# Scores of a half's last key tile from whole F32 operands in layer A's attention

## The chip, the core and the metric

The kernel runs on one core of one Trainium2 chip. The metric is the device time of one execution in microseconds (us); lower is better. Engines are named as the profile names them: PE (TensorE matmuls), PEld (TensorE weight loads), DVE (VectorE), ACT (ScalarE), POOL (GpSimd) and SP (SyncE, which here only issues DMAs).

## The reference

The program is a two-layer decoder trunk on one sequence of 1024 tokens, width 1024, in F32. Layer A is an mLSTM mixer, layer B a dilated sliding-window attention; the change lies in layer A. Cut to what is computed there (4 heads of width 512; b is the running sum of the log forget gates):

```
xc = silu(causal_dwconv(xm, conv_w, conv_b))
q = headwise(xc, wq); k = headwise(xc, wk); v = headwise(xm, wv)
sc  = einsum('bhld,bhsd->bhls', qc, kc) * w_intra      # causal, decayed by the gates
num = ... + einsum('bhls,bhsv->bhlv', sc, vc)
den = ... + sc.sum(-1)
h   = num / max(|den|, exp(-m))
y   = (group_norm(sigmoid(o) * h) * gn_g + skip * xc) * silu(z)
x   = layer_norm(ALPHA * x + y @ w_out)
```

The reference walks over the sequence in chunks with a carried state; the kernel computes the same as one causal attention over the 1024 tokens.

## The kernel before, in words

Almost every product of the kernel is made by `mm3` (lines 95 to 99): both operands have been split by `split` (lines 91 to 93) into a part h in the type fp32r (an ACT cast, line 92) and a rest l (a subtraction on DVE, line 93), and three matmuls h*h, h*l and l*h are added up in PSUM (lines 97, 98, 99). At some places of layer B the kernel instead gives TensorE whole F32 operands in one matmul instruction (lines 1240, 1242, 1290, 1321).

`layer_a_attend` is layer A's attention. It goes through 8 steps, (head, half) with 4 heads and 2 halves of 512 queries. A step has nj = 4 (first half) or 8 (second half) key tiles of 128 tokens. For each key tile j

- `scores` (line 787) multiplies, over the head's 4 channel tiles cc, the 128 keys (the conv output xc, split) with the queries (split; the weights of q and k are folded into the query side by `prep_q`). Because of causality only query columns from `lo * 128` on are needed, with lo = max(0, j - 4 * half): tiles of 512 columns, and at the end of each half one each of 384, 256 and 128 columns. Then ACT makes the exponentials (line 801), DVE multiplies (803), the result is split (805), and a running sum is kept (807, 809).
- `values` (line 812) multiplies the score tile with the values, 3 matmuls of 512 columns for each query block.

Scores run two key tiles ahead of values. At the end of a step `prep_q` (line 763) makes the next step's queries: for each of 4 channel tiles, three matmuls into PSUM bank 6 or 7, then the split from PSUM. `gather` and `norm` (lines 819, 830) finish the step's numerator, with 4 activations of ACT at line 854. `finish` (line 856) is called in the following step: it transposes h (line 867), scales the conv output in place by skip (ACT, line 869), adds the transposed h (DVE, line 870) and multiplies with the gate (POOL, line 871). The conv output that `finish` works on is a whole F32 copy, `self.xc`, one tile of 128 x 1024 for each of the 16 channel tiles; four of them are loaded at line 892, in each first half's iteration j == 1.

Tiles of SBUF are numbered slots; a slot's next user waits until the last reader of the one before has ended. Slots 50 and 51 are used before the attention (weights of the output gate) and after it (`w_raw` of `layer_a_out`, line 959: the raw tiles of w_out, loaded at line 964, turn about in 50 and 51). The attention itself does not use them.

The order of instructions on each engine, DMA issues on SP included, is fixed when the program is built: the tile framework's planner (line 1667, `schedule_with_timeline_sim=True`) takes the program order as priority, plays the program through with durations of its own, and lets an engine that would be idle go ahead with work that is later in the program. On the chip each engine follows the order so found and waits by semaphores.

Of the kernel before, what the change touches and what calls it, by code (L numbers as in the profile page):

```python
# [18 lines left out]
P = 128  # L19
# [6 lines left out]
HC = NC_A // HA  # L26
# [10 lines left out]
def f(ap):  # L37
    return ap.bitcast(F32)
# [22 lines left out]
class Kernel:  # L61
# [674 lines left out]
    def layer_a_attend(self):  # L736
        nc, cp = self.nc, self.cp
        V, A, G, T = nc.vector, nc.scalar, nc.gpsimd, nc.tensor
        xc_slots = ((40, 41, 42, 43), (8, 9, 10, 11))
        v_slots = (0, 1, 2, 3, 12, 13, 14, 15)  # L740
        q_slots = (44, 45, 46, 52)
        tos = Ring(7, 49)
        es, shl, hsl, pbs = Ring(5, 6), Ring(33, 34, 35), Ring(36, 37), Ring(4, 39)
        pS, pT = Ring(4, 5), Ring(6, 7)
# [1 line left out]
        xcs, vts, qs = {}, {}, {}  # L746

        def prep_x(hd, half, ccs=range(HC)):
            for cc in ccs:
                hl = self.slot(xc_slots[half][cc], (P, 2, 512), F32R)  # L750
                nc.sync.dma_start(f(hl), self.dram["xp", hd * HC + cc, half])
                xcs[hd, cc, half] = hl[:, 0], hl[:, 1]

        def prep_v(hd, half, js=range(4)):
            for j in js:
                j += 4 * half
                h, l = self.pair(v_slots[j])
                nc.sync.dma_start(f(l), self.dram["v", hd][j * P:j * P + P, :])
                self.nc.scalar.copy(h, f(l))
                G.tensor_tensor(l, f(l), f(h), op=ALU.subtract)  # L760
                vts[hd, j] = h, l

        def prep_q(hd, half):
            At = self.slot(48, (P, 2, 512), F32R)
            nc.sync.dma_start(f(At), self.dram["A", hd // 2][:, :, (hd % 2) * 512:(hd % 2) * 512 + 512])
            for cc in range(HC):
                ps = self.bank(pT)
                cs = slice(cc * P, cc * P + P)
                h, l = xcs[hd, cc, half]
                self.mm3(ps, At[:, 0, cs], At[:, 1, cs], h, l, True, True)  # L770
                qh, ql = self.pair(q_slots[cc])
                self.split(qh, ql, ps)
                qs[hd, cc, half] = qh, ql

        accs = {}
# [11 lines left out]
        def scores(hd, half, j, st):  # L787
            lo = max(0, j - 4 * half)
            ps = self.bank(pS)
            for cc in range(HC):  # L790
                kh, kl = xcs[hd, cc, j // 4]
                ks = slice((j % 4) * P, (j % 4) * P + P)
                qh, ql = qs[hd, cc, half]
                self.mm3(ps[:, lo * P:], kh[:, ks], kl[:, ks], qh[:, lo * P:], ql[:, lo * P:],
                         cc == 0, cc == HC - 1)
            e = self.slot(es, (P, 2, 512))
            E, sc = e[:, 0], e[:, 1]
            for i in range(lo, 4):
                ig = 4 * half + i
                src = st["pbm"] if ig == j else st["pb"]  # L800
                A.activation(E[:, i * P:i * P + P], src[:, i * P:i * P + P], AF.Exp, bias=self.bias[:, hd, ig, j:j + 1])  # L801
            cs = slice(lo * P, 512)
            V.scalar_tensor_tensor(sc[:, cs], ps[:, cs], SCALE_A, E[:, cs], op0=ALU.mult, op1=ALU.mult)
            sh, sl = self.pair(shl)
            self.split(sh[:, cs], sl[:, cs], sc[:, cs])
            if j == 0:
                V.tensor_copy(st["acc"], sc)
            else:
                (G if half else V).tensor_tensor(st["acc"][:, cs], st["acc"][:, cs], sc[:, cs], op=ALU.add)
            return lo, sh, sl  # L810

        def values(hd, half, j, st, sc):
            lo, sh, sl = sc
            vh, vl = vts[hd, j]
            for i in range(lo, 4):
                ts = slice(i * P, i * P + P)
                self.mm3(st["num"][i], sh[:, ts], sl[:, ts], vh, vl, j == 0, j == 4 * half + i)
# [38 lines left out]
        def finish(hd, half, st, c2):  # L856

            sz = self.slot(38, (P, 2, 512))
            for ii in range(2):
                c = hd * HC + 2 * c2 + ii  # L860
                self.last_load = nc.sync.dma_start(sz[:, ii], self.dram["z", c][:, 512 * half:512 * half + 512])
            for ii in range(2):
                cc = 2 * c2 + ii
                c = hd * HC + cc
                pt = self.bank(pT)
                for i in range(4):
                    T.transpose(pt[:, i * P:i * P + P], st["h"][i][:, cc * P:cc * P + P], self.ident)  # L867
                xcv = self.xc[c][:, 512 * half:512 * half + 512]
                A.activation(xcv, xcv, AF.Copy, scale=self.skip[:, c:c + 1])
                V.scalar_tensor_tensor(xcv, pt, self.gng[:, c:c + 1], xcv, op0=ALU.mult, op1=ALU.add)  # L870
                G.tensor_tensor(xcv, xcv, sz[:, ii], op=ALU.mult)  # L871
# [11 lines left out]
        for n, (hd, half) in enumerate(steps):  # L883
            st["num"] = [self.bank(i) for i in range(4)]
            nj = 4 * half + 4
            last = n + 1 == len(steps)
            nxt = None
            for j in range(nj):
                if j == 1 and half == 0:
                    for c in range(HC * hd, HC * hd + HC):  # L890
                        t = self.slot((20, 21, 22, 23, 24, 25, 26, 27, 16, 17, 18, 19, 28, 29, 30, 31)[c])
                        nc.sync.dma_start(t, self.dram["xc", c])
                        self.xc.append(t)
                if j + 2 < nj:
                    ahead.append(scores(hd, half, j + 2, st))
                if not last:
                    if half == 0 and j < 2:
                        prep_x(*steps[n + 1], (2 * j, 2 * j + 1))
                        prep_v(*steps[n + 1], (2 * j, 2 * j + 1))
                    if half and j in (2, 3):  # L900
                        prep_x(*steps[n + 1], (2 * j - 4, 2 * j - 3))
                    if half and j in (4, 5):
                        prep_v(*steps[n + 1], (2 * j - 8, 2 * j - 7))
                    if j + 2 == nj:
                        prep_q(*steps[n + 1])
                values(hd, half, j, st, ahead.pop(0))
                if prev and j in (2, 3):
                    finish(*prev, j - 2)
            gather(hd, half, st)
            if not last:  # L910
                nst = begin(*steps[n + 1])
                ahead.append(scores(*steps[n + 1], 0, nst))
            norm(hd, half, st)
            prev = hd, half, st
            if not last:
                ahead.append(scores(*steps[n + 1], 1, nst))
                st = nst
# [753 lines left out]
```

## Time and profile before

| | us |
|---|---|
| three timed runs | 2014.91, 2022.83, 2025.81 |
| their median | 2022.83 |
| the profiled execution, its own time | 2016.23 |
| its span, first to last instruction | 2014.5 |
| PE busy in the span | 1963.6 (97%) |
| DVE busy | 1444.0 (72%) |
| ACT busy | 993.1 (49%) |
| POOL busy | 154.0 (8%) |

How to read it: the span is cut into instructions with a start, a duration and, where an engine stood idle before one, what released it. [...] The profile names tiles without numbers: `s` is any slot, `b` any PSUM bank, `dc` the scratch copy of the conv output. A helper's line stands for all its callers; so most matmuls are on lines 97 to 99, casts on 92 and subtractions on 93. The attention's steps lie between about 500 and 790 us, and the projection with w_out follows.

### The profile page before, as it was taken

To read this page: it belongs to the slowest core of one execution; us is meant where nothing else is said; L and a number is where in the kernel's file an instruction comes from. 1 tells how busy PE (TensorE), PEld (TensorE's weight loads), DVE (VectorE), ACT (ScalarE), POOL (GpSimd) and SP (SyncE) were. 2 spreads that over 40 slices of the span, in tenths; PEclk is the share of its full clock that TensorE was granted. 3 is DMA by queue.
4 is the path that set the end of the run, shared out by engine and by line. 5 is a ranking of instruction groups with operands and counts; after the bars stand their busy time and mean duration, and the time that the engine had idled before them with its cause. 6 is when DMAs were issued, how large, how long until landed. Compare 5 with 4: busy or idle time off the path is not lost.

```text
span 2014.5 us, 26553 instructions
## 1 busy us (share of the span) xinstructions
PE 1963.6 (97%) x9512; PEld 1627.5 (81%) x9512; DVE 1444.0 (72%) x2851; ACT 993.1 (49%) x1988; POOL 154.0 (8%) x127
## 2 busy tenths in 40 slices
PE   8999999999999999999999999999999999999997
PEld 6788888788888888878788888877887788888776
DVE  8778787675467776457867765776568987776888
ACT  5455555535645543343524542565255456675621
POOL 0110000012145343000000000000000000000000
PEclk9999999999999999999999999999999999999999
DMA  4345465456754543516121143125335632224753
GB/s 170 133 168 199 160 219 183 151 164 237 269 204 158 198 157 113 185 63 241 53 74 52 54 149 112 66 102 178 109 104 196 235 105 84 85 95 149 274 199 126
DMA packets 116477, 300.65 MB, mean 149 GB/s; under 512 B 13493, under 2 KB 31349, under 8 KB 116345
## 3 DMA queue, kind: packets, MB, share of 16 engines
q1 hardware_dynamic: 116344, 298.95, 42.5%
q8 instruction: 75, 1.23, 0.2%
q14 instruction: 58, 0.47, 0.1%
HBM read 206.32 MB, written 92.59 MB: 148 GB/s over the span
## 4 chain that ended last, share of the span: by engine, by line
PE 76%; DVE 12%; DMA 6%; ACT 3%; issue 2%; SPq 0%; POOL 0%; DVEq 0%; ACTq 0%
PE b L97 23%; PE b L99 23%; PE b L98 23%; DVE s L93 3%; PE b L592 1%; ACT s L92 1%; DMA s<-df 1%; PE b L1267 1%; DMA s<-in_w_qk 1%; DVE s L230 1%; DVE s L141 1%; PE b L598 1%; PE b L867 1%; DVE s L1406 1%; PE b L1290 1%
## 5 line engine op out<-in xcount | busy, mean ns | idle before, releaser
L98 PE MATMUL b<-s,s 128*128 128x512 f32 (+3 forms) x2720 | 1036.8, 383 | 2.1 <-DVE s L93 2.1
L99 PE MATMUL b<-s,s 128*128 128x512 f32 (+3 forms) x2720 | 1023.5, 383 | 6.0 <-DVE s L93 6.0
L97 PE MATMUL b<-s,s 128*128 128x512 f32 (+2 forms) x2720 | 1003.6, 387 | 25.7 <-ACT s L92 21.9
L93 DVE TENSOR_TENSOR s<-s,s 128x512 fp32r<-128x512 f32 (+2 forms) x702 | 508.2, 739 | 285.9 <-ACT s L92 280.3
L92 ACT CAST s<-s 128x512 fp32r<-128x512 f32 (+3 forms) x706 | 436.0, 638 | 544.2 <-PE b L99 316.5
L97 PEld LDWEIGHTS b<-s,s 128*128 128x128 f32 x2720 | 512.8, 189 | 130.5 <-ACT s L92 30.0
L99 PEld LDWEIGHTS b<-s,s 128*128 128x128 f32 x2720 | 511.7, 189 | 108.1 <-DVE s L93 11.5
L98 PEld LDWEIGHTS b<-s,s 128*128 128x128 f32 x2720 | 513.7, 189 | 99.4 <-DVE s L93 4.4
L230 DVE TENSOR_TENSOR s<-s,b 128x512 f32<-128x512 f32 x132 | 89.9, 682 | 31.9 <-PE b L99 30.5
L1253 ACT ACTIVATE s<-s,nmax 128x128 f32<-128x128 f32 (+1 forms) x192 | 84.4, 441 | 44.0 <-DVE nmax L1251 43.6
L93 DVE TENSOR_TENSOR s<-b,s 128x512 fp32r<-128x512 f32 (+1 forms) x96 | 51.6, 553 | 34.9 <-ACT s L92 31.2
L557 DVE SCALAR_TENSOR_TENSOR s<-s,c_convw,s 128x512 f32<-128x512 f32 (+3 forms) x96 | 71.2, 753 | 3.5 <-ACT s L554 3.2
L224 DVE TENSOR_TENSOR s<-s,b 128x512 f32<-128x512 f32 x88 | 59.6, 680 | 17.3 <-PE b L99 12.6
L314 DVE TENSOR_TENSOR s<-s,b 128x512 f32<-128x512 f32 x100 | 63.2, 680 | 8.0 <-PE b L99 6.2
L801 ACT ACTIVATE s<-s,k 128x128 f32<-128x128 f32 x144 | 47.2, 392 | 42.3 <-DVE s L93 19.3
L310 DVE TENSOR_TENSOR s<-s,s 128x1024 f32<-128x1024 f32 x40 | 49.7, 1246 | 19.9 <-DMA s<-in_w_o 9.9
L1249 DVE CUSTOM_DVE_ANT_0 s<-b,k 128x128 f32<-128x128 f32 (+1 forms) x192 | 57.2, 344 | 7.5 <-PE b L99 5.5
L243 DVE TENSOR_TENSOR s<-s,s 128x512 f32<-128x512 f32 x44 | 30.3, 689 | 42.9 <-DMA s<-in_w_qk 20.5
L92 ACT CAST s<-b 128x512 fp32r<-128x512 f32 (+1 forms) x96 | 43.9, 480 | 24.1 <-PE b L99 13.7
L760 POOL TENSOR_TENSOR s<-s 128x512 fp32r<-128x512 f32 x32 | 43.7, 1381 | 76.7 <-DMA s<-dv 45.5
L1200 DVE SCALAR_TENSOR_TENSOR s<-s,s 128x512 fp32r<-128x512 f32 x48 | 42.4, 884 | 9.9 <-ACT s L1199 9.5
L871 POOL TENSOR_TENSOR s<-s,s 128x512 f32<-128x512 f32 x32 | 42.7, 1351 | 64.5 <-DVE s L870 48.8
(179 smaller groups left out, 1476.6 us busy)
## 6 DMA issues: line engine op xcount, KB each, us to landing
s<-in_w_qk SPq DMA_DIRECT2D x48, 512.0 KB
s<-in_w_out SPq DMA_DIRECT2D x40, 512.0 KB
dp<-s SPq DMA_DIRECT2D x32, 512.0 KB
s<-dp SPq DMA_DIRECT2D x32, 512.0 KB
s<-in_w_z SPq DMA_DIRECT2D x24, 512.0 KB
s<-in_w_v SPq DMA_DIRECT2D x24, 512.0 KB
dg<-s SPq DMA_DIRECT2D x24, 512.0 KB
s<-dg SPq DMA_DIRECT2D x24, 512.0 KB
```

The source lines that it names most:

```text
L92: self.nc.scalar.copy(h, src)
L93: self.last_split = (l_eng or self.nc.vector).tensor_tensor(l, src, f(h), op=ALU.subtract)
L97: mm(ps, lh, rh, start=start, stop=False, skip_group_check=skip)
L98: mm(ps, lh, rl, start=False, stop=False, skip_group_check=skip)
L99: mm(ps, ll, rh, start=False, stop=stop, skip_group_check=skip)
L224: V.tensor_tensor(o, p, q, op=add)
L230: V.tensor_tensor(o, p[lane][rows], q[lane][rows], op=add)
L310: eng.tensor_tensor(o[j], p[j], q[j], op=op)
L314: V.tensor_tensor(o, p, q, op=add)
L557: V.scalar_tensor_tensor(u[i][:, lo:o + 512], xm[i][:, lo - s:o + 512 - s], convw[:, c, 3 - s:4 - s], u[i][:, lo:o + 512], op0=ALU.mult, o ...
L1249: V.tensor_tensor_reduce(out=dst, in0=sc, in1=bias, op0=ALU.add, op1=ALU.max, scale=1.0, scalar=-3e38, accum_out=mx[:, b:b + 1])
L1253: self.last_exp = A.activation(res[b][0], res[b][0], AF.Exp, bias=nm[:, b:b + 1], accum_out=stat[:, 1, g, b:b + 1])
```

## The change

The last key tile of each half, the one with 128 query columns (lo == 3), is no longer computed by `mm3` from split operands. For each of the 4 channel tiles one matmul multiplies the whole F32 keys, read from `self.xc`, with a whole F32 copy of the last 128 query columns. That copy is new: `prep_q` writes it from PSUM by one ACT copy of 128 x 128 after each channel tile's split, into a tile in slots 50 and 51, turn about by step. Because the whole keys must be there earlier, the four loads of line 892 are put into iteration j == 0. All other score tiles stay as they were.

```diff
-        q_slots = (44, 45, 46, 52)
+        q_slots, q_whole = (44, 45, 46, 52), Ring(50, 51)
...
             nc.sync.dma_start(f(At), self.dram["A", hd // 2][:, :, (hd % 2) * 512:(hd % 2) * 512 + 512])
+
+            qs[hd, half] = self.slot(q_whole, (P, HC, P))
             for cc in range(HC):
...
                 self.split(qh, ql, ps)
+                nc.scalar.copy(qs[hd, half][:, cc], ps[:, 384:512])
                 qs[hd, cc, half] = qh, ql
...
                 qh, ql = qs[hd, cc, half]
+                if lo == 3:
+                    T.matmul(ps[:, 384:512], self.xc[hd * HC + cc][:, j * P:j * P + P], qs[hd, half][:, cc],
+                             start=(cc == 0), stop=(cc == HC - 1))
+                    continue
                 self.mm3(ps[:, lo * P:], kh[:, ks], kl[:, ks], qh[:, lo * P:], ql[:, lo * P:],
                          cc == 0, cc == HC - 1)
...
-                if j == 1 and half == 0:
+                if j == 0 and half == 0:
                     for c in range(HC * hd, HC * hd + HC):
```

## The prediction

> **What bounds the kernel now.** I read the page's busy table first, then the stretches around the attention, then who waited for whom on PE there, and last the timelines at the places that those name. From the page, the waits between 470 and 830 us, and two stretches (a first-half step and what follows the last score tile; columns: length, then busy us and count of PE, PEld, DVE, ACT, POOL, the granted clock, the DMA share and GB/s):
>
> ```profile
> PE 1963.6 (97%) x9512; PEld 1627.5 (81%) x9512; DVE 1444.0 (72%) x2851; ACT 993.1 (49%) x1988; POOL 154.0 (8%) x127
> ```
> ```profile
> PE b L97 <- ACT s L92: 3.9, 5, 0.9
> ```
> ```profile
> 665.10:712.90 47.80, 46.97 (x241) 39.13 (x240) 35.15 (x77) 25.75 (x59) 23.61 (x19) 1.00 0.40 138
> 775.20:800.00 24.80, 23.88 (x127) 19.83 (x126) 14.73 (x41) 4.91 (x7) 7.96 (x7) 1.00 0.28 94
> ```
>
> PE is the bound, in the attention too: it is busy for 46.97 of 47.80 us at full clock, while ACT has half its time free. What PE loses there is a handful of waits, 3.9 us in five, all for an ACT cast. So the change must be judged by two things: how much PE time a score tile costs, and what happens to those few waits.
>
> **The tile's price.** The first row of the old tile and the two rows behind its last, and the nearest relative of the new one, a group of whole F32 matmuls in layer B (start, duration):
>
> ```profile
> 541.65 0.23 PE L97 MATMUL b<-s,s 128*128 128x128 f32 x1
> ...
> 542.94 0.45 PE L97 MATMUL b<-s,s 128*128 128x512 f32 x1
> 543.23 0.39 PE L98 MATMUL b<-s,s 128*128 128x512 f32 x1
> ```
> ```profile
> 1497.18 0.39 PE L99 MATMUL b<-s,s 128*128 128x512 f32 x1
> 1497.41 1.05 PE L1321 MATMUL b<-s,s 128*128 128x128 f32 x8
> 1498.21 0.48 PE L97 MATMUL b<-s,s 128*128 128x512 f32 x1
> 1498.53 0.40 PE L98 MATMUL b<-s,s 128*128 128x512 f32 x1
> ```
> ```profile
> L1321 PE MATMUL b<-s,s 128*128 128x128 f32 x128 | 16.8, 274 | 0.0
> ```
>
> A 512-column matmul in a stream takes 0.23 us (1497.18 to 1497.41). The old tile's 12 matmuls run from 541.65 to 542.94; the 512-column matmul behind them takes 0.29 instead of 0.23, so they cost 1.29 + 0.06 = 1.35 us. Line 1321 is executed 64 times (8 heads, 2 banks, 4 products), and the profile counts 128: a whole F32 matmul leaves two records. The x8 is thus one bank's four products, as many as the new tile has: 1497.41 to 1498.21, and the matmul behind takes 0.32, so 0.80 + 0.09 = 0.89 us. Both come to 0.11 us for each record. The saving is 1.35 - 0.89 = 0.46 us a tile; there is one such tile in each of 8 steps, so 3.7 us of PE time, which is 0.18%.
>
> [...]
>
> **What of it stays.** PE's waits of the first-half steps, one of them with its chain (the chain of waits, in order of time; the x1 of line 97 is the score tile in question):
>
> ```profile
> 553.49 0.97 PE L97 MATMUL b<-s,s 128*128 128x512 f32 x3 [0.81 <-ACT s L92]
> 604.28 0.50 PE L97 MATMUL b<-s,s 128*128 128x512 f32 x1 [0.92 <-ACT s L92]
> 675.22 0.50 PE L97 MATMUL b<-s,s 128*128 128x512 f32 x1 [0.83 <-ACT s L92]
> 738.50 0.50 PE L97 MATMUL b<-s,s 128*128 128x512 f32 x1 [0.83 <-ACT s L92]
> ```
> ```profile
> 665.11 0.22 PE L97 MATMUL b<-s,s 128*128 128x128 f32 x1
> ```
> ```profile
> 661.37 0.80 PE b L834 x8
> ...
> 670.15 0.28 DVE s L803
> ...
> 670.88 1.28 ACT s L801 x4
> 672.15 2.83 ACT s L854 x4
> 674.98 0.20 ACT s L92
> 675.18 0.04 issue
> 675.22 0.50 PE b L97
> ```
>
> Step (2, 0)'s last tile is on PE from 665.11, over by about 666.5, and waits in its bank until DVE comes to it at 670.15: DVE works off the norm that PE released at 661.37, ACT then does four exponentials and the four activations of line 854, and only then the cast on which PE waits. A tile that ends 0.46 us earlier moves none of this; PE merely waits 0.46 us longer. So steps (1, 0), (2, 0) and (3, 0), where the chain starts at the norm each time, keep nothing. The four second-half tiles are different: behind each of them PE runs without a wait to the next norm, and the next chain starts at that norm. They keep 4 x 0.46 = 1.84 us.
>
> Step (0, 0) has another chain:
>
> ```profile
> 533.42 1.32 ACT s L869 x2
> 534.74 1.04 ACT s L652 x2
> ...
> 539.46 7.60 DMA do<-s
> ...
> 550.52 2.45 ACT s L801 x8
> ```
> ```profile
> L869 ACT ACTIVATE s<-s,c_skip x32: 706/712/727, 486.8 to 546.1; 128x512 f32<-128x512 f32 x32
> L892 SPq DMA_DIRECT2D s<-dc x16: 320/380/1122, 482.9 to 536.8; - x16
> ```
>
> All 32 in-place scalings of line 869 are done before 546.8, far ahead of their program order, as soon as the copies of line 892 have landed. With the change a scaling may not run before the score tile that reads the unscaled keys, so all 32 move behind their tiles. The chain of step (0, 0) then loses the pieces of line 869 ahead of line 652: 1.3 us in this chain, out of which come at most two of the new copies. I count the wait of 0.81 and the tile's 0.46 as saved here, 1.27 us; the bounds are 0 and 1.27.
>
> **What it adds.** Copies: 4 a step, 32 in all. The nearest row is a copy of the same size from PSUM:
>
> ```profile
> L1278 ACT COPY pw<-b x48: 258/267/376, 1094.6 to 1816.7; 128x128 f32<-128x128 f32 x40, 128x256 f32<-128x256 f32 x8
> ```
>
> So 4 x 0.267 = 1.07 us of ACT a step. The bank is not held longer: the subtraction from PSUM begins when the cast ends and is the longer of the two. The moved scalings bring 4 x 0.71 = 2.85 us a step. In the stretch from 665.10 ACT is busy for 25.75 of 47.80 us, so the 7.8 us of two steps fit in; but ACT works in its fixed order, and before the casts of steps (1, 0) to (3, 0) it has PE waiting. Bounds for each of these three: nothing, if the new work stands in ACT's gaps, and 1.07 + 2.85 = 3.9 us, if all of it stands ahead of the cast and no gap takes any. I take one copy, 0.27, near the lower end, since the scalings are the lowest in priority there and the gaps in that stretch are
>
> ```profile
> 668.39 0.69 ACT L801 ACTIVATE s<-s,k 128x128 f32<-128x128 f32 x2 [1.84 <-DVE s L93]
> 669.40 0.40 ACT L801 ACTIVATE s<-s,k 128x128 f32<-128x128 f32 x1 [0.31 <-DVE s L93]
> 670.88 1.28 ACT L801 ACTIVATE s<-s,k 128x128 f32<-128x128 f32 x4 [0.66 <-DVE s L93]
> ```
>
> 2.81 us together, about four scalings. That is +0.8 us.
>
> The loads of line 892 cost nothing where they go: SP issues them by 536.8, the first reader is the tile at 541.65, the others come later. Their move past a step's loads of keys and values is one in the program only, as SP has them ahead of these already. The second-half tile reads columns 896 to 1023, `finish` of the first half writes 0 to 511: no wait.
>
> Slots 50 and 51 cost something of another kind. Now the first two w_out tiles are loaded into them ahead of the attention; with the change the first must wait for step (3, 0)'s last tile, ahead of the wait at 738.50, and the second for step (3, 1)'s:
>
> ```profile
> 497.20 0.33 SPq L964 DMA_DIRECT2D s<-in_w_out  x1
> 501.59 0.33 SPq L964 DMA_DIRECT2D s<-in_w_out  x1
> ```
> ```profile
> 776.47 0.27 PE L99 MATMUL b<-s,s 128*128 128x128 f32 x1
> 796.22 1.03 PE L867 MATMUL b<-c_ident,s 128*128 128x128 f32 x8
> ```
> ```profile
> L92 ACT CAST s<-s 128x1024 fp32r<-128x1024 f32 x4 | 4.2, 1052 | 1.8 <-PE b L99 1.8
> ```
>
> PE goes through the first three w_out tiles, 18 matmuls each, right before the transposes at 796.22, so it needs the second at 796.22 - 36 x 0.23 = 787.9, or 2 us earlier by the savings. A 512 KB transfer took 7.60 us in the chain above, the cast 1.05: 776.7 + 7.6 + 1.05 = 785.4. It just fits; I take 0, with 0 to 2 us as bounds. What is queued behind that load on SP are later w_out tiles, whose parts go into slots that the attention holds to its end.
>
> **The sum.** -1.84 - 1.27 + 0.8 = -2.3 us: 2016.23 - 2.3 = 2013.9 for an execution like the profiled one. That one lies 6.6 us below the median; on the median it is 2022.83 - 2.3 = 2020.5, 0.11% down. About 0.5%, 10 us, is what a measurement of this kernel can tell from no change.
>
> **The rivals.**
> *ACT's order (slower).* The copies and scalings of a step stand ahead of the cast for which PE waits, in all four first-half steps: 4 x 3.9 = 15.7 us, less the 1.84 kept: +13.8, 2036.7. It decides once more than the 2.81 us of gaps is put in front of the cast. For it speaks that ACT is in these chains already, against it the low priority. 0.08.
>
> [...]
>
> *All waits gone (faster).* With ACT free of the scalings until 542 and PE ahead, the planner finds an order without the four waits: -3.7 - 3.4 = -7.1, 2015.7. 0.14.
>
> [...] 0.03.
>
> *Another order elsewhere.* The planner sees other durations and may reorder later stages, or the second w_out tile comes late: a few us either way, seldom 10. 0.15.
>
> The forecast has 0.60. The runs before spread over 10.9 us, so even there a median may stray past 10 us: 0.04 of the 0.60 and 0.04 of the 0.14 I count as faster, with 0.02 of the other orders: faster 0.10. Slower: 0.07 of the first rival and 0.03 of the other orders, 0.10. The rest, 0.80, is within 0.5%. The range: the lowest run less 2.3 is 2012.6, less 7.1 is 2007.8; the highest less 2.3 is 2023.5, with four passes 2029.8. I take 2009 to 2030; most of the first rival is left out.
>
> **What would show it.** Right: 64 records of whole matmuls in the attention with about 0.11 us each, 8 groups of 0.8 us from first start to the next; line 869 spread over the steps up to 790; PE's wait at 553 gone, those near 604, 675 and 738 between 0.9 and 1.6; the second w_out load right after the last tile, and no PE wait before the first transposes of the tail. Wrong: a tile over 1.3 us; a PE wait of several us behind a cast in first-half steps; PE waiting for w_out near 785; or a difference that lies after 830, where nothing was changed but the order.

## The result, and the profile after

The changed kernel takes 2025.96 us (median of 22 runs, 2022.05 to 2032.75), the kernel before 2021.74 beside it (22 runs, 2014.91 to 2027.49). The ratio is 1.0024, with a 95% interval of 1.0015 to 1.0034: slower by about 4.9 us, where 2.3 us less were forecast.

The tile became what was forecast. From the timeline of PE in the kernel after (start, duration), and its group (count, busy us, mean ns):

```profile
544.59 1.06 PE L798 MATMUL b<-s,s 128*128 128x128 f32 x8
545.40 0.47 PE L97 MATMUL b<-s,s 128*128 128x512 f32 x1
545.72 0.39 PE L98 MATMUL b<-s,s 128*128 128x512 f32 x1
```
```profile
L798 PE MATMUL b<-s,s 128*128 128x128 f32 x64 | 9.1, 274 | 0.0
```

Four products leave 8 records and take 0.81 us from first start to the next; the matmul behind takes 0.32 instead of 0.23. (The prices are distances of starts, because the records of neighbours overlap: the one at 545.72 is 0.39 us long, and the next starts at 545.95.) That is 0.90 us for a tile, against the 0.89 forecast, and 64 records in all.

So the time must be lost elsewhere, and it is lost in the attention. The norm of the last step starts at 791.53 us, before it was 785.74 (in a second trace of the kernel before 788.99). The stretch from 480 to 880 us holds the attention and what follows at once. Its row for the kernel before, for the second trace of that, and for the kernel after (length, busy us and count of PE, PEld, DVE, ACT, POOL, granted clock, DMA share, GB/s):

```profile
480.00:880.00 400.00, 395.15 (x1937) 331.48 (x1936) 259.31 (x516) 191.10 (x381) 119.92 (x95) 1.00 0.53 184
```
```profile
480.00:880.00 400.00, 394.70 (x1932) 330.62 (x1931) 259.50 (x513) 192.35 (x386) 122.73 (x97) 1.00 0.52 182
```
```profile
480.00:880.00 400.00, 390.68 (x1883) 324.67 (x1882) 242.99 (x508) 195.12 (x413) 120.10 (x95) 1.00 0.53 182
```

PE stands idle for 9.3 us of these 400, where it stood for 4.9 and 5.3. The waits that the prediction named (553, 604, 675, 738) are gone. In their place, from PE's timeline after, each with what ended the idle time:

```profile
542.39 0.48 PE L97 MATMUL b<-s,s 128*128 128x512 f32 x1 [2.15 <-ACT s L92]
...
600.62 0.67 PE L97 MATMUL b<-s,s 128*128 128x512 f32 x2 [0.73 <-ACT s L92]
...
659.34 0.91 PE L97 MATMUL b<-s,s 128*128 128x512 f32 x3 [0.70 <-ACT s L92]
...
666.94 0.50 PE L97 MATMUL b<-s,s 128*128 128x512 f32 x1 [1.07 <-DMA s<-dA]
...
725.89 0.92 PE L97 MATMUL b<-s,s 128*128 128x512 f32 x3 [0.69 <-ACT s L92]
...
729.77 0.68 PE L97 MATMUL b<-s,s 128*128 128x512 f32 x2 [0.99 <-ACT s L92]
```

From 600 us on these are no longer the waits for the split of a score tile after the norm. They stand in the making of the next step's queries, and in four of these five PE goes on when ACT has cast a query: at 659.34, 0.05 us after the end of the cast that starts at 658.71. (The one at 666.94 is for the load of the query weights.) What ACT does around 659, first before, then after:

```profile
654.76 0.62 ACT L759 CAST s<-s 128x512 fp32r<-128x512 f32 x1 [2.72 <-DMA s<-dv]
655.29 0.58 ACT L92 CAST s<-b 128x512 fp32r<-128x512 f32 x1
...
656.65 0.57 ACT L92 CAST s<-b 128x512 fp32r<-128x512 f32 x1
657.78 0.59 ACT L92 CAST s<-b 128x512 fp32r<-128x512 f32 x1 [0.56 <-PE b L99]
659.70 0.59 ACT L92 CAST s<-b 128x512 fp32r<-128x512 f32 x1 [1.33 <-PE b L99]
661.90 0.62 ACT L759 CAST s<-s 128x512 fp32r<-128x512 f32 x1 [1.61 <-DMA s<-dv]
```
```profile
656.22 0.56 ACT L92 CAST s<-b 128x512 fp32r<-128x512 f32 x1
658.18 0.62 ACT L759 CAST s<-s 128x512 fp32r<-128x512 f32 x1 [1.40 <-DMA s<-dv]
658.71 0.58 ACT L92 CAST s<-b 128x512 fp32r<-128x512 f32 x1
659.19 0.27 ACT L775 COPY s<-b 128x128 f32<-128x128 f32 x1
660.09 0.62 ACT L759 CAST s<-s 128x512 fp32r<-128x512 f32 x1 [0.63 <-DMA s<-dv]
...
663.60 0.27 ACT L775 COPY s<-b 128x128 f32<-128x128 f32 x1 [0.59 <-DVE s L93]
```

Before, the four query casts (`s<-b`) stand together, and ACT waits for PE. After, casts of the values (line 759), which wait for their loads, and the new copies stand between them, and PE waits for ACT. The copies wait too. The group over the attention (us in total, times, longest):

```profile
ACT s L775 <- DVE s L93: 5.5, 13, 0.9
```

In this trace none of the 32 copies begins before DVE's subtraction from the same bank has ended, and ACT's queue stands with it: 16 of them begin 0.03 us after that end, the others later. The one at 663.60, for instance, follows a subtraction that runs from 662.88 for 0.69 us. What keeps the two from running side by side was not shown.

The last piece is the clock. The stretch after those waits, and matmuls in it:

```profile
660.00:670.00 10.00, 8.90 (x41) 7.03 (x40) 5.95 (x18) 3.86 (x9) 3.06 (x3) 0.87 0.44 155
670.00:680.00 10.00, 10.00 (x52) 8.62 (x52) 5.38 (x19) 9.27 (x24) 1.40 (x1) 0.96 0.07 26
```
```profile
668.03 0.63 PE L97 MATMUL b<-s,s 128*128 128x512 f32 x1
668.45 0.63 PE L98 MATMUL b<-s,s 128*128 128x512 f32 x1
668.88 0.63 PE L99 MATMUL b<-s,s 128*128 128x512 f32 x1
```

At a granted clock of 0.87 and 0.96 these 20 us lose 10 x 0.13 + 10 x 0.04 = 1.3 + 0.4 = 1.7 us by estimate; the matmuls stand 0.43 us apart instead of 0.23. In the trace of before no stretch between 480 and 880 had less than 1.00.

To add this up, a stretch of equal work is needed: from the start of ACT's first split of a query (526.84 and 529.23 us before, 527.46 after) to the start of DVE's first row of the product with w_out (861.21 and 864.81, 866.92). Its rows for the kernel before, the second trace of that, and the kernel after:

```profile
526.84:861.21 334.37, 329.52 (x1647) 277.11 (x1646) 219.71 (x451) 154.81 (x319) 115.70 (x92) 1.00 0.50 175
529.23:864.81 335.58, 330.28 (x1647) 277.27 (x1646) 220.31 (x452) 154.73 (x319) 116.67 (x92) 1.00 0.50 175
527.46:866.92 339.46, 330.14 (x1615) 274.54 (x1614) 209.49 (x451) 173.71 (x375) 116.17 (x93) 0.99 0.51 175
```

After, it is 3.9 to 5.1 us longer, which is about the whole loss; what follows it takes 1153.3 and 1156.0 us before and 1155.0 after. PE's idle time in it rises by 4.2 us (9.3 against the mean of 4.9 and 5.3), and the clock takes 1.7. PE's busy time without the clock's 1.7 us falls only by 1.1 to 1.8 us (to 328.4), where eight tiles should spare 8 x 0.45 = 3.6 us. What took the other 2 us or so of busy time was not found.

### The profile page after: what moved, and what is told of

Same layout as the page of the kernel before. It is cut to its first block, busy times and chain, and to the rows that moved or that the text cites. A ratio compares the mean times of both kernels' runs of the same rounds, so it can differ in the third digit from the quotient of the medians.

```text
span 2021.9 us, 26520 instructions
## 1 busy us (share of the span) xinstructions
PE 1966.1 (97%) x9480; PEld 1626.3 (80%) x9480; DVE 1433.3 (71%) x2851; ACT 996.8 (49%) x2020; POOL 154.0 (8%) x127
## 4 chain that ended last, share of the span: by engine, by line
PE 74%; DVE 12%; DMA 9%; ACT 2%; issue 2%; SPq 0%; POOL 0%; DVEq 0%; ACTq 0%
PE b L97 23%; PE b L99 23%; PE b L98 23%; DVE s L93 3%; DMA s<-in_w_out 1%; PE b L592 1%; DMA s<-df 1%; ACT s L92 1%; DMA s<-in_w_qk 1%; PE b L1274 1%; DMA ds<-s 1%; DMA s<-dv 1%; PE b L598 1%; DVE s L1256 1%; PE b L874 1%
## 5 line engine op out<-in xcount | busy, mean ns | idle before, releaser
L98 PE MATMUL b<-s,s 128*128 128x512 f32 (+3 forms) x2688 | 1029.1, 385 | 5.0 <-DVE s L93 4.7
L97 PE MATMUL b<-s,s 128*128 128x512 f32 (+3 forms) x2688 | 999.9, 389 | 29.2 <-ACT s L92 25.0
L99 PE MATMUL b<-s,s 128*128 128x512 f32 (+3 forms) x2688 | 1014.7, 384 | 4.9 <-DVE s L93 4.8
L92 ACT CAST s<-s 128x512 fp32r<-128x512 f32 (+2 forms) x706 | 435.9, 638 | 568.2 <-PE b L99 343.4
L97 PEld LDWEIGHTS b<-s,s 128*128 128x128 f32 x2688 | 507.0, 189 | 135.8 <-ACT s L92 34.8
L98 PEld LDWEIGHTS b<-s,s 128*128 128x128 f32 x2688 | 508.3, 189 | 104.7 <-DVE s L93 10.0
L99 PEld LDWEIGHTS b<-s,s 128*128 128x128 f32 x2688 | 505.7, 189 | 106.8 <-DVE s L93 9.6
L314 DVE TENSOR_TENSOR s<-s,b 128x512 f32<-128x512 f32 x100 | 63.0, 680 | 12.2 <-PE b L99 10.7
```

The costliest lines, as they stand in the source:

```text
L92: self.nc.scalar.copy(h, src)
L97: mm(ps, lh, rh, start=start, stop=False, skip_group_check=skip)
L98: mm(ps, lh, rl, start=False, stop=False, skip_group_check=skip)
L99: mm(ps, ll, rh, start=False, stop=stop, skip_group_check=skip)
L314: V.tensor_tensor(o, p, q, op=add)
```

## The experiments

Two kinds of theory stood against each other. By one, a part that the change adds costs the time by itself: the copies, the scalings that now wait for their tiles, the moved loads, the slots. By the other, the parts cost little, and the time is lost by the order that the planner makes of the changed program: what stands ahead of what in ACT's queue. The change and all eighteen runs made after it, each as a ratio to the kernel before on the same chip:

| run | ratio | 95% interval |
|---|---|---|
| the change | 1.0024 | 1.0015 to 1.0034 |
| before_again: the kernel before | 1.0006 | 0.9993 to 1.0020 |
| copies: before, with the copies unread | 1.0008 | 0.9997 to 1.0020 |
| loads_j0: before, with the loads moved | 1.0008 | 0.9996 to 1.0021 |
| vpool_before: before, value casts on POOL | 1.0002 | 0.9990 to 1.0014 |
| tile_alone: before, with the tile alone | 1.0021 | 1.0013 to 1.0030 |
| tile_pinned: the same, ACT's order tied | 0.9995 | 0.9984 to 1.0007 |
| own_keys: change, scalings set free | 1.0031 | 1.0015 to 1.0047 |
| own_space: change, slots 50 and 51 free | 1.0001 | 0.9992 to 1.0010 |
| q_first: change, value casts behind | 1.0027 | 1.0016 to 1.0038 |
| act_order: change, all casts tied | 1.0030 | 1.0018 to 1.0043 |
| copy_dve: change, copy by DVE | 1.0012 | 1.0001 to 1.0024 |
| pool_add: change, sum by POOL | 1.0001 | 0.9991 to 1.0012 |
| vpool_after: change, value casts on POOL | 0.9995 | 0.9983 to 1.0006 |
| copy_first: change, copy ahead of the split | 0.9989 | 0.9980 to 0.9998 |
| copy_first_2: the same once more | 0.9998 | 0.9988 to 1.0009 |
| early_a: copy_first, weights loaded early | 1.0010 | 0.9999 to 1.0021 |
| vpool_first: copy_first, value casts on POOL | 0.9985 | 0.9976 to 0.9994 |
| vpool_first_2: the same once more | 0.9988 | 0.9977 to 0.9999 |

### The parts, one by one

**copies.** The kernel before with the buffers and the copies; nothing reads them.

```diff
+            qs[hd, half] = self.slot(q_whole, (P, HC, P))
...
+                nc.scalar.copy(qs[hd, half][:, cc], ps[:, 384:512])
```

> The 32 ACT copies of the last query columns and their slots 50 and 51 are added to the kernel before; the score tile stays three products of parts and nothing reads the copies; the scalings may run early as before. Copy theory (the copy waits for DVE's subtraction from the same PSUM bank, holds ACT and the bank, and so slows the making of the queries): slower than before by what the change lost in all, 4.9 us net plus the 3.7 us of PE time that it saved, so +6 to +9 us. Scaling theory (the 32 in-place scalings that had to move behind the score tiles fill ACT's queue): within 1.5 us of before. Order theory (the planner's new order of casts, loads and query groups, which any edit can set off, costs the time): anywhere from -5 to +8 us, and the copies themselves need not be where PE waits.

1.0008: 1.6 us, and the interval holds one. By themselves the copies don't make up the loss.

**pool_add.** The change with the whole query put together by POOL out of its two parts in SBUF (so the operand is the sum of the parts, not the value in PSUM), and no copy by ACT.

```diff
-                nc.scalar.copy(qs[hd, half][:, cc], ps[:, 384:512])
+                G.tensor_tensor(qs[hd, half][:, cc], f(qh[:, 384:512]), f(ql[:, 384:512]), op=ALU.add)
```

> The changed kernel, but the whole query columns are put together from their two parts by POOL, in SBUF, instead of being copied out of PSUM by ACT. Copy theory: the loss goes and the saving of the tiles shows, -2 to -4 us against before. Scaling theory: the scalings are still in the attention, so +4 to +6 us as in the changed kernel. Order theory: no sign fixed, and PE's waits lie elsewhere than in the changed kernel.

1.0001: the loss is gone, the 3.7 us of the tiles don't show.

**own_keys.** The change with the tile's keys loaded into a tile of their own (4 loads of 64 KB a step), so that the scalings need not wait for the tile; the loads of `self.xc` are back in iteration 1.

```diff
+            for cc in range(HC):
+                nc.sync.dma_start(qk[:, 1, cc], self.dram["xc", hd * HC + cc][:, 512 * half + 384:512 * half + 512])
...
-                    T.matmul(ps[:, 384:512], self.xc[hd * HC + cc][:, j * P:j * P + P], qs[hd, half][:, cc],
+                    T.matmul(ps[:, 384:512], kw[hd, half][:, cc], qs[hd, half][:, cc],
```

> The changed kernel, but the score tile reads its keys from a copy of its own (four loads of 64 KB a step, beside the query copy), and the loads of the conv output are back in iteration 1; the scalings of the conv output wait for no score tile and may run early again. Copy theory: still slower, +4 to +6 us against before. Scaling theory: -2 to -4 us, and line of the scaling again done before 550 us. Order theory: no sign fixed.

1.0031: the scalings run early again (the last begins at 549.5 us, before it was 546.1), and the loss stays. They are not the cause, though the four loads a step that this run adds may have a price of their own.

**loads_j0.** The kernel before with the loads moved, nothing else.

```diff
-                if j == 1 and half == 0:
+                if j == 0 and half == 0:
```

> The kernel before with one edit: the loads of the conv output stand in iteration 0 instead of 1. No work is added or taken away. Copy theory and scaling theory: within 1 us of before. Order theory: the planner's order changes all the same, and the time moves by 1 to 5 us, either way.

1.0008, not to be told from nothing.

**own_space.** The change with the copies' buffers outside the slots, so that the first two w_out tiles are loaded ahead of the attention again.

```diff
-            qs[hd, half] = self.slot(q_whole, (P, HC, P))
+            qs[hd, half] = self.t(cp, [P, HC, P], tag="qwhole", bufs=2)
```

> The changed kernel with the copies' buffers in space of their own, so that slots 50 and 51 take the first two w_out tiles ahead of the attention again. If the late w_out load costs: 1 to 2 us under the changed kernel, and that after 780 us alone. If not, as I predicted: the same within 1 us, with the norm starts as in the changed kernel to within the order's scatter.

1.0001, 4.6 us under the change, more than either theory had. The trace does not put it where w_out is used: the last norm starts at 788.09, 3.4 us earlier than in the change, and the first norm is 1.1 us earlier already. Of the 3.4 us the clock makes 1.7, as no stretch between 480 and 880 has less than 1.00 in this trace; PE's busy time from 480 to 880 rises only from 390.68 to 391.75. What the slots cost is not settled; that it is 0 to 2 us, as forecast, is not confirmed.

### The tile alone, and ACT's order

**tile_alone.** Only the tile is changed, with operands that are there already: the high parts read as whole F32. The low parts' contribution to this tile is left out. No copies, no new waits, no moved loads.

```diff
+                if lo == 3:
+                    T.matmul(ps[:, 384:512], f(kh[:, ks]), f(qh[:, 384:512]), start=(cc == 0), stop=(cc == HC - 1))
+                    continue
```

> The kernel before with the tile's twelve products replaced by four whole F32 products of what is there already (the high parts of keys and queries read as F32; the low parts' contribution to this tile is left out). No copies, no slots, loads and in-place scalings as before. If the tile's saving of 0.46 us lands at all: 1.8 to 3.7 us under the kernel before, norm starts 0.46 us earlier after each second-half tile, the waits of about 0.8 us at the first-half casts as they were. If the saving only turns into longer waits or another order: within 1 us of the kernel before, with more PE waiting for ACT casts in the attention. If whole products cost more than 0.11 us a record in a stream: slower by 0.5 us a tile, 4 us.

1.0021: the tile alone loses 4.2 us, almost as much as the whole change, though it spares PE 0.46 us eight times. A theory of added parts cannot explain that. PE's order is nearly that of the kernel before; ACT's differs in four places. Two of PE's waits, and what ACT does ahead of the first:

```profile
683.44 1.23 PE L97 MATMUL b<-s,s 128*128 128x512 f32 x3 [1.98 <-ACT s L92]
...
738.59 0.50 PE L97 MATMUL b<-s,s 128*128 128x512 f32 x1 [1.89 <-ACT s L92]
```
```profile
678.63 0.28 ACT L92 CAST s<-s 128x128 fp32r<-128x128 f32 x1
678.82 2.93 ACT L857 ACTIVATE s<-s,nb,ray 128x512 f32<-128x512 f32 x4
681.66 1.26 ACT L804 ACTIVATE s<-s,k 128x128 f32<-128x128 f32 x4
682.83 1.04 ACT L92 CAST s<-b 128x512 fp32r<-128x512 f32 x2
```

The kernel before has these at the same place (its lines 801 and 854 are 804 and 857 above, 808 and 861 in the changed kernel, 809 and 865 in tile_pinned):

```profile
673.48 1.50 ACT L854 ACTIVATE s<-s,nb,ray 128x512 f32<-128x512 f32 x2
674.88 0.28 ACT L92 CAST s<-s 128x128 fp32r<-128x128 f32 x1
675.07 1.06 ACT L92 CAST s<-b 128x512 fp32r<-128x512 f32 x2
676.03 1.28 ACT L801 ACTIVATE s<-s,k 128x128 f32<-128x128 f32 x4
```

There the four exponentials stand behind the first two query casts, here ahead of them, and PE waits 1.15 us longer (1.98 against 0.83).

**tile_pinned.** The same kernel with three rules that put ACT's casts back into the order of the kernel before, for the heads from the second on. That is three of the four places; the one in the first step, near 546 us, stays.

```diff
+            with self.tc.issue_after(self.last_norm.ins) if pin and lo == 3 else ExitStack():
+                self.split(sh[:, cs], sl[:, cs], sc[:, cs])
...
+                with self.tc.issue_after(self.tile_cast.ins) if hd and half and cc == 0 else ExitStack():
+                    self.split(qh, ql, ps)
...
+            with self.tc.issue_after(self.q_cast.ins) if hd and half and j == 1 else ExitStack():
```

> The new tile by itself once more (whole F32 products of the high parts; the low parts' contribution to that tile is left out), with ACT's order tied to that of the kernel before by three rules for the heads from the second on: the last tile's cast stands behind the four activations of the norm, the first query cast behind that cast, and the exponentials of the next step's second tile behind the second query cast. Without the ties ACT took these in another order (last tile's cast first, the next tile's exponentials ahead of the query casts) and it was 4 us slower than before. If that order is the cause of the loss: PE's waits near 597, 683 and 738, 2 us each, go back to about 0.8, PE stands idle for 7 to 9 us between 480 and 910 instead of 15, and the time is 0 to 4 us under the kernel before. If whole products cost something by themselves, or the order of PE or DVE is the cause: 3 to 5 us over the kernel before, as without the ties.

0.9995: the two intervals (0.9984 to 1.0007, and 1.0013 to 1.0030) don't meet. The order of a few instructions on ACT is worth 5.2 us here, more than the tile saves. PE's and DVE's order in the attention differ between the two programs in one place each, near 617 us. At the same place as above:

```profile
676.52 2.92 ACT L865 ACTIVATE s<-s,nb,ray 128x512 f32<-128x512 f32 x4
679.35 0.28 ACT L92 CAST s<-s 128x128 fp32r<-128x128 f32 x1
679.53 1.06 ACT L92 CAST s<-b 128x512 fp32r<-128x512 f32 x2
680.49 1.28 ACT L809 ACTIVATE s<-s,k 128x128 f32<-128x128 f32 x4
```
```profile
679.68 0.50 PE L97 MATMUL b<-s,s 128*128 128x512 f32 x1 [0.84 <-ACT s L92]
```

The wait is back at the 0.83 of the kernel before. Not all came back: a wait of 2.99 us for DVE near 605 stayed, and PE's busy time from 480 to 880 rose from 386.91 to 389.73 only. The stretch of equal work is 342.6 us in the trace of tile_alone and 338.1 in that of tile_pinned, 4.5 us less (1.7 of them the clock), but 334.4 and 335.6 in the kernel before. So the trace does not show why tile_pinned as a whole is no slower than the kernel before; it is the trace of the lowest of its 12 executions.

**q_first.** The change, with three of the values' casts put behind the fourth query cast, as they stood before.

```diff
+                with self.tc.issue_after(q_cast[hd, 0].ins) if hd and j > 4 else ExitStack():
+                    self.nc.scalar.copy(h, f(l))
```

> The changed kernel with one rule more for ACT: the second to fourth cast of the second half's values stand behind the fourth query cast of the step, as they did in the kernel before. The rest of the order stays nearly as it was in the changed kernel. If these casts, waiting for their loads between the query casts, are the cause: PE's waits near 659, 723, 726 and 730 go or shrink below 0.3 us, and the time is 2 to 5 us under the changed kernel, that is within 0 to 3 us of the kernel before. If it is something else that POOL's taking over of all the value casts mended: within 1.5 us of the changed kernel, 3 to 6 us over the kernel before.

1.0027: this theory falls. The wait at 659 shrank from 0.70 to 0.26, but what PE gained there it lost a little later to the load of the query weights, 3.9 us in three waits where there was 1.1 in one:

```profile
PE b L97 <- DMA s<-dA: 3.9, 3, 1.8
PE b L97 <- ACT s L92: 3.7, 5, 1.6
```

**act_order.** q_first, and the three rules of tile_pinned as well (the second for all four query casts).

> The changed kernel with ACT's order tied to that of the kernel before in all four places: the three casts of values behind the query casts, the last tile's cast behind the norm's four activations, the query casts of the second half behind that cast, the next step's second exponentials behind the second query cast. Copies and scalings stay where the planner puts them. If it is the order of these casts alone: 2 to 5 us under the changed kernel, within 0 to 3 us of the kernel before. If the copies and scalings cost the time by standing in ACT's queue wherever they are put: within 2 us of the changed kernel, 3 to 6 us over the kernel before.

1.0030: tying the casts does not mend the change as it mends the tile alone. PE's waits for the load of the query weights are 3.9 us in three again, as in q_first. The run tests the tied places and not the whole order: copies and scalings apart, ACT's queue still differs from that of the kernel before (near 632 us, for one, four exponentials stand ahead of a score tile's cast that was ahead of them), and PE's and DVE's order largely remain those of the change.

### Taking work out of ACT's way

**copy_first.** The copy ahead of the split, so that no instruction of ACT waits for DVE's subtraction.

```diff
-                self.split(qh, ql, ps)
                 nc.scalar.copy(qs[hd, half][:, cc], ps[:, 384:512])
+                self.split(qh, ql, ps)
```

> The changed kernel with the copy of the query's last 128 columns issued ahead of the split, so that ACT does copy, cast and nothing on ACT waits for DVE's subtraction from the bank. If ACT standing in its queue behind that subtraction (5.5 us of waits in 13) is what delays the next casts: the waits of ACT line 775 for DVE go, PE's wait for casts in the attention falls from 6.3 to about 4 us, and the time is 2 to 5 us under the changed kernel. If the bank's hold time is the cause: no change, since copy, cast and subtraction hold it just as long; within 1 us of the changed kernel. If the planner's order is: anything within 3 us either way, with the waits in other places.

0.9989, 7 us under the change by the ratios (5 by that of the repetition). The waits of the copies for DVE are gone, and PE is busy nearly as long as before:

```profile
480.00:880.00 400.00, 394.03 (x1913) 329.78 (x1912) 257.48 (x522) 196.15 (x416) 120.08 (x95) 1.00 0.54 184
```
```profile
PE b L97 <- DMA s<-dA: 2.8, 3, 1.1
PE b L97 <- ACT s L92: 1.7, 3, 0.7
```

This does not part the two theories, because the bank is held for a shorter time as well: from the start of a bank's first reader to the end of its last it is 1.5 us on average in the kernel before (32 query tiles), 2.5 us in the change and 1.7 us here. And neither the waits nor the hold is a price by itself. ACT's waits for DVE ahead of the copies (5.5 us in the change) are in copies, vpool_after and own_space:

```profile
ACT s L775 <- DVE s L93: 10.7, 21, 0.9
ACT s L775 <- DVE s L93: 8.7, 17, 0.9
ACT qwhole L775 <- DVE s L93: 5.3, 14, 0.8
```

The ratios of these three are 1.0008, 0.9995 and 1.0001, and the last two hold the bank for 2.3 and 2.5 us. The order on PE and DVE is another in copy_first, too. So the run shows that the loss can be taken back with the copy still on ACT, but not which of these differences does it.

**copy_dve.** The copy by DVE behind its subtraction.

```diff
-                nc.scalar.copy(qs[hd, half][:, cc], ps[:, 384:512])
+                V.tensor_copy(qs[hd, half][:, cc], ps[:, 384:512])
```

> The changed kernel with the copy made by DVE behind its own subtraction, so that ACT has no copy at all; DVE gets 32 more instructions of about 0.2 us. If ACT's standing in its queue is the cause: PE's wait for casts falls to about 4 us and the time is 3 to 5 us under the changed kernel, as with the sum made by POOL. If the hold of the bank is: no better than the changed kernel, 0 to 2 us over it, since DVE is busy 72 per cent and its copy still stands behind the subtraction.

1.0012: half of the loss. It lies between the two theories and decides little.

**vpool_before** and **vpool_after.** The casts of the values by POOL instead of ACT, in the kernel before and in the changed one.

```diff
-                self.nc.scalar.copy(h, f(l))
+                G.tensor_copy(h, f(l))
```

> The kernel before with the 32 casts of the values made by POOL instead of ACT, as the pair for the next run. ACT is relieved of 32 x 0.62 us and of the waits for the values' loads; POOL, busy for 8 per cent, gets about 32 x 1.3 us more. If these casts cost nothing in the kernel before, where they stand behind the query casts: within 2 us of it. POOL may be late with the values: then slower by several us, with PE waiting for POOL at the start of a step's value products.

> The changed kernel with the same move. If the changed kernel loses its time because the values' casts, waiting for their loads, stand between the query casts in ACT's queue: PE's waits at about 600, 659, 723 and 726 go, and it is 3 to 6 us under the changed kernel and 1 to 4 us under the kernel before with the same move. If ACT's copies behind DVE's subtraction, or the order as a whole, are the cause: within 2 us of the changed kernel, and 3 to 6 us over its pair.

1.0002 and 0.9995. The kernel before gains nothing, the changed one 0.29%, and the change is now 0.07% faster than its pair, which is within what ratios repeat to. With q_first this speaks against the place of these casts and for ACT's having less in its queue around the queries; it does not prove it, since the planner has ordered everything else anew as well.

**early_a.** copy_first with the load of the query weights issued a step earlier.

```diff
+                    if j == 0:
+                        load_a(*steps[n + 1])
```

> The changed kernel with the copy ahead of the split, which was 0.11 per cent under the kernel before, and with the load of a step's query weights issued at the start of the step before, since three of the waits left there (2.8 us in all) are for that load. If the load was issued too late: those three waits go and the time is 1 to 3 us less, 3 to 5 us under the kernel before. If the load stands in SP's queue behind loads that wait for their slots, or another order comes out: no better than within 2 us of the kernel before.

1.0010. In its trace PE is busy for 396.37 of the 400 us, the most of all kernels, and the time is no better for it. The trace is of its lowest execution (2013.37 of 2013.37 to 2028.08). Why the others are longer is open.

**vpool_first** and its repetition, the version that came out best: copy_first and vpool_after together.

> The changed kernel with both remedies: the copy ahead of the split, and the casts of the values made by POOL. If each takes waits off ACT's queue by itself and the tile's saving of 3.7 us is then kept: 2 to 5 us under the kernel before. If they mend the same waits, or each new order brings waits of its own: 0 to 2 us under it.

> The kernel with both remedies once more, copy ahead of the split and value casts by POOL, since the copy ahead of the split alone gave 0.11 per cent in one run and 0.02 in the next. If its gain is real: 2 to 4 us under the kernel before with one outside the interval again. If it was chance: within 1.5 us of it.

0.9985 and 0.9988: 3.0 and 2.4 us under the kernel before, with one outside both intervals. It is faster than both kernels, than the kernel before by most of the 3.7 us of the tiles, and vpool_before shows that the POOL casts alone give nothing.

### How far one program differs from itself

> The kernel with the copy ahead of the split once more, since its gain of 0.11 per cent is near what the interval can tell. If the gain is real: 1 to 4 us under the kernel before, with the same order and so the same PE waits in its trace to within 0.5 us each. If it was chance: within 1 us of it.

> The kernel before, unchanged, as a run of its own. If the intervals tell what they say: ratio 1.000 with one inside the interval, and the same waits as in its first trace, since the order is fixed. If executions of one program differ by their transfers: PE's waits in the attention differ by 1 us or more in all, though the order is the same.

copy_first gave 0.9989 and then 0.9998, the kernel before 1.0006 against itself. So ratios repeat to about 0.1%, and a single 0.1% proves little. The traces show one reason. Ten microseconds of copy_first, in its first trace and in its second:

```profile
600.00:610.00 10.00, 9.18 (x52) 7.71 (x52) 9.67 (x29) 6.74 (x16) 3.18 (x3) 1.00 0.23 83
```
```profile
600.00:610.00 10.00, 10.00 (x44) 9.05 (x45) 8.21 (x22) 5.67 (x15) 3.74 (x3) 0.66 0.16 60
```

The order is the same, but in one execution the granted clock falls to 0.66, which costs 3.4 us by the same estimate (10 x 0.34). The two spans are 2014.5 and 2020.4 us. The waits differ as well, by more than the 0.5 us that was expected: near 599 us PE waits for an ACT cast for 0.59 us in the first trace and 1.62 in the second, and near 667 it waits 1.09 us for the query weights in the first alone. In the two traces of the kernel before PE's idle time between 480 and 880 differs by 0.4 us.

## Why the prediction was wrong, point by point

- **The tile's price** was right: 0.90 us measured, 0.89 forecast. So was the number of records, 64 for 32 products. No run shows the four passes that stand in the forecast's range (2029.8) and behind its chance of 0.03; the runs show two records a product, and 0.225 us for a product of the new tile (0.90 / 4). That is 3.9 times the 0.057 us that 128 columns would take at the rate of a 512-column matmul (0.23 / 4, an estimate). It is the old tile that is dear: the three-product matmuls of the kernel before stand 0.23, 0.175, 0.12 and 0.11 us apart (medians) at 512, 384, 256 and 128 columns, so the last halving saves almost nothing.
- **What stays of it** is the step that failed, and this decided the sign. It said of the first-half chains that "A tile that ends 0.46 us earlier moves none of this", and of the second-half tiles that "They keep 4 x 0.46 = 1.84 us". Both take the order of the kernel before, and with it its waits, as given. But the order is made anew from the changed program. In the change the four waits named are gone, and others, in the making of the next step's queries and at 542 us, leave PE idle for 4.2 us more; the clock takes 1.7 us. tile_alone shows that the tile by itself costs 4.2 us through the new order, and tile_pinned that three places in ACT's queue account for 5.2.
- **The copies** were mis-sized and misjudged. The prediction added one copy of 0.27 us for each of three steps, 0.8 us, and said "The bank is not held longer: the subtraction from PSUM begins when the cast ends and is the longer of the two". The trace shows the copy behind the subtraction, with 5.5 us of ACT's waits, and the bank held for 2.5 us instead of 1.5. What of the 4.9 us the copies cost is open: runs with as long waits or holds lose little or nothing (copies, vpool_after, own_space).
- **Step (0, 0)**: the wait at 553 went, as said, but one of 2.15 us came at 542, so the 1.27 us were not kept.
- **The scalings** were taken at next to nothing, and setting them free brought nothing (own_keys). They are spread over the steps, up to 782.5. **The loads** cost nothing that can be measured (loads_j0).
- **The w_out tiles**: PE has no wait of several us near 785, as said; own_space leaves open whether the slots cost something earlier.
- **A reading**: not all of PE's waits there were for a cast. Two more, 0.7 and 0.2 us near 798 us, were for DVE; they are in the kernel after as well, so nothing hangs on them.
- **The rivals**: the first had the right engine and the wrong load. It put the copies and scalings ahead of the casts after the norm and reckoned 13.8 us; 4.9 us came, the scalings are not the cause, and the waits are elsewhere. The second had its condition fulfilled, the four waits gone, and not its gain, because others came. The last had the right cause, another order, with 0.15, and looked for it elsewhere; it stood in the attention itself.

What is shown: the tile's saving is real and most of it can be kept (vpool_first, twice), and the order that the planner gives ACT can take it away (tile_alone against tile_pinned). What is argued: that in the change, too, it is what stands in ACT's queue around the queries. copy_first, pool_add and vpool_after, which take work or waits out of that queue, lose nothing, but each is a new order on every engine. What is open: a single instruction that costs the change its time. Tying the casts did not mend it (q_first, act_order), and own_space mended it without touching the copies' place or their waits.

## What to carry to other kernels

Where a planner lays out the queues, a change of 0.46 us in one tile is also a change of order, so first ask of a small saving which queue is nearly late and what might be put ahead of its urgent instructions. In the change the copies out of a PSUM bank stood behind DVE's reading of it, and ACT's queue with them (5.5 us in 13 waits). The copy was better ahead of that reader (0.9989 and 0.9998 against 1.0024), yet with the copy behind it, and longer waits (8.7 us), vpool_after lost nothing (0.9995), so the place has to be tried. Nor did waits in ACT's queue set the time by themselves: in copies they came to 10.7 us, at 1.0008. And a difference of 0.1% needs a second run of the same kernel before it is believed.

## What the runs showed of the hardware that was not expected

- The granted clock falls for short stretches, with matmuls 0.43 us apart instead of 0.23, in another number in each execution: summed over the 10-us stretches of the first 2000 us they take 6.8 and 10.2 us in the two traces of the kernel before, 6.8 and 15.3 in those of copy_first. Between 480 and 880 us they showed in none of five traces with the old tile and in ten of fifteen with the new one, 1.7 or 3.4 us each time. In the change they follow a string of waits of PE, but waits of 2.15 us (the change itself, at 542) and 2.25 us (vpool_before) passed without one; what starts them is open.
- POOL casts a tile of 128x512 to fp32r in 0.66 us (vpool_first), nearly as little time as ACT, where 1.3 were expected:

```profile
L759 POOL CAST s<-s 128x512 fp32r<-128x512 f32 x32 | 21.0, 662 | 60.4 <-DMA s<-dv 60.3
```

  ACT needs 0.62 for the same cast (the rows of line 759 in the fences of ACT's casts above), while POOL's subtraction of that size takes 1.40 (line 760 there). (The profile's durations on POOL are rough.)
